# Second layer of a two-layer encoder kernel: another order of the attention units, the output projection begun with other rows, three numbers of the planner changed

## Chip, cores and metric

The kernel runs on one core of a Trainium2 chip. The metric is the time of one execution in device microseconds (us); lower is better. The time before is the median of three runs.

## The reference, cut to what matters

Two token sequences (1024 and 512 real tokens, each with 16 meta tokens in front, so 1040 and 528 rows, 1568 in all) go through two layers of width 1024 in float32:

```python
def layer(x, ...):
    h = rmsnorm(x, pre_g)
    proj = einsum('bld,de->ble', h, w_in)             # 1024 -> 3328 columns
    aq, ak, av, ag, bq, bk, bv, bg = parts
    oa = window_gqa_attention(rope(aq), rope(ak), av, sink) * silu(ag)   # 8 heads, 2 groups
    ob = diff_attention(rope(bq), rope(bk), bv, lam, ...) * silu(bg)     # 4 heads of 2 softmaxes
    o = einsum('ble,ed->bld', concatenate([oa, ob], axis=-1), w_out)
    return x + rmsnorm(o, post_g)
```

Sliding attention (`oa`): 8 query heads in 2 groups share a key head per group; a query sees the 16 meta tokens, keys up to 128 positions away on either side, and a sink. Differential attention (`ob`): 4 heads, each the difference of two full softmaxes over the whole sequence, applied to values of width 128, then normalised per row. The mixed rows are 512 of sliding and 512 of differential attention; the output projection multiplies all 1024 with `w_out`.

## The kernel before, in words

Every matmul works on float32 numbers split into a high and a low part, so each product is three matmuls. Tokens are cut into four chunks of 392; the input projection has 26 blocks of 128 columns. A differential head needs four blocks (two of queries and keys, values, gate); sliding group 0 needs six (keys and values of both groups among them), group 1 four.

A layer has six **units**: differential heads b0 to b3, `attn_b`, and sliding groups a0 and a1, `attn_a`. `units[0..3]` are the heads, `units[4]` and `units[5]` the groups. `UNITS[l]` gives the order in layer l. The main loop records, for each unit in that order, first its attention and then the input projection (`inproj`) of the unit that comes next: so dense matmuls of the next unit stand beside the attention of this one. After the last unit `outproj` is recorded. Its steps stand in `OUT_ORDER`: `first` (letter b) multiplies one half of the mixed rows with `w_out` for all chunks and keeps the partial sums; `second` (s, or S with weights not kept) adds the other half, then normalises, adds the residual and stores. `FH[l]` says which half `first` takes: 0 is the sliding rows, 1 the differential rows. Each half is 4 column blocks x 12 token tiles x 12 matmuls = 576 matmuls in layer 1.

Results pass between steps through DRAM: `AQ`, `AK`, `AV` (sliding queries, keys, values), `BS`, `BV` (differential), `GT` (gates), `MX` (mixed rows). All transfers are issued from one queue, SP's.

Nothing of this order is final. A `Recorder` writes every instruction down as an `Op` with a number `prio` (its place in the recording, less a boost and less a base), and `schedule()` deals them out to the engines beforehand: whenever an engine is free, it takes the ready op of lowest `prio`. What runs on the chip is that fixed order on each engine. `BASE[l]` holds the bases of the output projection's steps by their letter, `BASE_A[l]` those of the attention units by their place in the order (not by the unit); in layer 1 it is `(0, 0, 0, 0, 1500, 300)`, so places 5 and 6 are drawn forward.

Some ops can run on either of two engines (`any_copy`: ScalarE or VectorE; `any_tt`: VectorE or GpSimd). They stand on both lists, and `ANY` is added to their `prio` on one engine's list:

```python
def push(o):
    for e in o.alts:
        heapq.heappush(ready[e], (o.prio + (ANY[e] if len(o.alts) > 1 else 0), o.seq, o))
```

Buffers that matter: `slot` (16; the normalised input of the four chunks fills all of them as high and low parts until the last input projection has read it; then the mixed rows and the partial sums of `first` use them), `kk` and `vv` (one each: keys and values of a sequence; the next unit's can only be loaded when this one's are done), `qq` (2), `pp` (4), `whl` (2, split weights), and the PSUM pools `ps_s` (1: scores), `ps_t` (2), `ps_o` (1), `ps_d` (2: dense). With weights kept, `second` puts two of its four weight blocks into `kk` and `vv`, behind the last op of the last attention unit (`after[0]`). In the attention units the buffers of `ps_s`, `kk`, `qq`, `vv`, `pp`, `at`, `og` and `gl` are taken in recorded order, so units do not overtake each other.

In the trace all instructions have line L448, the line of the planner that issues them; tiles tell what they are.

Of the kernel before, what the change touches and what calls it, by code (L numbers as in the profile page):

```python
# [54 lines left out]
SPARE = (0, 0)  # L55
GROUPS = (((0, 1), (2, 3)), ((0, 1), (2, 3)), ((0, 1), (2, 3), (4, 5)))
COMB = ((1, 1, 1, 1), (1, 1, 1, 1))
BASE = ({'f': 400, 'p': 100, 's': -100, 'S': 0, 'b': 800, 'g': -50}, {'f': 0, 'S': 400, 'l': 1000})
BASE_A = ((-200, 1500, 1500, -200, 200, 400), (0, 0, 0, 0, 1500, 300))
FH = (1, 1)  # L60
UNITS = ((0, 1, 2, 3, 4, 5), (0, 1, 2, 3, 4, 5))


def even_tiles(t0, n, m):
# [57 lines left out]
ENG = ("PE", "ACT", "DVE", "POOL", "SP")  # L122
PE_COL = 0.0004453
PE_SWITCH = 0.39
ANY = {'PE': 0, 'ACT': 20, 'DVE': 0, 'POOL': 0, 'SP': 0}
POOL_MAX = 300


# [107 lines left out]
class Recorder:  # L236
# [89 lines left out]
    def schedule(self):  # L326
# [16 lines left out]
# [4 lines that stand above are left out]
# [193 lines left out]
def hymba_kernel(ctx, tc, xT, xr, w_in, w_out, rope, masks, pre_g, post_g, sub_g, sink_b, sink_m, lam_in, yo):  # L540
# [244 lines left out]
    def load_w(src, pool=None, pri=0):  # L785
        nc.boost = BOOST_W + pri * 100000
        nc.extra = [after[0]] if pool and after else []
        raw = (p_p if pri or pool and after else wraw_p)([128, 1024])
        dma(raw, src)
        nc.boost = BOOST_W  # L790
        w = (pool or whl_p)([128, 2, 8, 128], F32R)
        rv = raw.rearrange("p (a c) -> p a c", a=8)
        nc.any_copy(w[:, 0], rv)
        nc.any_tt(w[:, 1], rv, f32(w[:, 0]), ALU.subtract)
        nc.extra = []
        nc.boost = 0
        return w
# [502 lines left out]
    def load_mix(l, ci, half, small=False):  # L1300
        nc.boost = BOOST_M
        his, los = [], []
        k = 2 if small else 4
        n = sum(m for _, m in OCH[ci])
        for r0 in range(4 * half, 4 * half + 4, k):
            if ci == 4:
                hi, lo = [at_p([128, 4, n], F32R) for _ in range(2)]
            else:
                hi, lo = [p_p([128, 2, CN], F32R) for _ in range(2)] if small else pair(F32R)
            o = 0  # L1310
            nc.extra = [after[0]] if small else []
            for (t0, m) in OCH[ci]:
                dma(lo[:, :, o:o + m], SC[l]["MX"][r0:r0 + k, :, t0:t0 + m].rearrange("e p t -> p e t"))
                o += m
            nc.extra = []
            nc.any_copy(hi[:, :, 0:n], f32(lo[:, :, 0:n]))
            nc.any_tt(lo[:, :, 0:n], f32(lo[:, :, 0:n]), f32(hi[:, :, 0:n]), ALU.subtract)
            his.append(hi)
            los.append(lo)
        nc.boost = 0  # L1320
        return rows(his, k), rows(los, k)
# [4 lines left out]
    def outproj(l):  # L1326
# [18 lines left out]
        def first(*cs_):  # L1345
            for ci in cs_:
                mix[ci] = load_mix(l, ci, FH[l])
                if ci < 4:
                    part[ci] = halves([128, 3, 512])
            for dp in range(4):  # L1350
                w = load_w(w_out[l, FH[l], dp])
                u, c0 = dp // 2, 256 * (dp % 2)
# [16 lines left out]
        def load(ci):  # L1369
            mix[ci, 1] = load_mix(l, ci, 1 - FH[l], ci == 3 and l > 0)  # L1370

        def second(*cs_, keep=True):
# [9 lines left out]
            def get(dp):  # L1382
                if dp not in kept:
                    w = load_w(w_out[l, 1 - FH[l], dp], (None, None, k_p, v_p)[dp] if keep else None)
                    if keep:
# [95 lines left out]
        for step in OUT_ORDER[l].split():  # L1481
            nc.base = BASE[l].get(step[0], 0)
            for c in ([step[1:]] if step[0] in "bsS" else step[1:] or [""]):
# [41 lines left out]
    for l in range(NL):  # L1525
        order = [units[u] for u in UNITS[l]]
        es = [(e, pool, START.get(f"w{i}", 0) if l == 0 else 0)
# [70 lines left out]
```

## Time and profile before

| | |
|---|---|
| time, median of 3 runs | 1920.6 us (1920.0 to 1920.7) |
| time of the profiled execution | 1922.3 us |
| its span, first to last instruction | 1920.5 us |
| TensorE (PE) busy in the span | 1840.4 us, 96% |
| VectorE (DVE) busy | 1487.8 us, 77% |
| ScalarE (ACT) busy | 1028.0 us, 54% |
| mean granted clock of TensorE | 0.99 |

The span is what the trace covers; the time has 1.8 us more around it. The first layer takes about the first half. In layer 1 the differential heads run to about 1562 us, the sliding groups from about 1578 to 1838, and the second half of the output projection from there to the end. PE is matmuls, PEld the weight loads that run beside them, SP the queue that issues transfers; a number in brackets behind a timeline row is idle time of the engine before it and what ended it.

### The profile page before, as it was taken

The page shows a single profiled execution, that of the slowest core. Times are in us where ns is not written, and L with a number is a line of the kernel's source. Part 1 is how long each engine was busy: PE and PEld are TensorE (multiplying, and loading weights), DVE is VectorE, ACT ScalarE, POOL GpSimd, SP SyncE. Part 2 cuts the span into 40 slices and gives each one's busy share as a digit, 9 for nine tenths or more (in the row PEclk, how much of TensorE's full clock was granted, in tenths as well). Part 3 has the DMA queues.
Part 4 walks back from the last instruction along what each step waited for, and adds up shares of the span by engine and source line. Part 5 has one row for each costly group of instructions (what it writes and reads, how often), then busy time and mean ns, then how long its engine had stood idle before and what let it go on. Part 6 is the DMA issues. An engine that isn't in the chain of part 4 may idle for free.

```text
span 1920.5 us, 35745 instructions
## 1 busy us (share of the span) xinstructions
PE 1840.4 (96%) x12400; PEld 1772.5 (92%) x12400; DVE 1487.8 (77%) x3353; ACT 1028.0 (54%) x2458; POOL 267.7 (14%) x521
## 2 busy tenths in 40 slices
PE   7999999999999998998799999999999999989998
PEld 7999999999999898898699999999999999889998
DVE  7577787888796887676987387887968859879777
ACT  8345454465554666565664255454546537658642
POOL 2011111212121110010220021111211111101101
PEclk9999999999999998999899999999999999999999
DMA  8444453634545665655454444445453475684374
GB/s 252 133 107 125 132 135 110 165 84 131 155 101 148 158 163 135 148 140 147 154 182 115 134 119 136 130 118 156 109 167 107 125 174 127 157 221 115 84 238 150
DMA packets 296498, 273.04 MB, mean 142 GB/s; under 512 B 100822, under 2 KB 259670, under 8 KB 296190
## 3 DMA queue, kind: packets, MB, share of 16 engines
q1 hardware_dynamic: 296318, 270.76, 51.0%
q8 instruction: 99, 1.62, 0.4%
q14 instruction: 81, 0.66, 0.1%
HBM read 149.19 MB, written 96.01 MB: 128 GB/s over the span
## 4 chain that ended last, share of the span: by engine, by line
PE 72%; DMA 10%; DVE 9%; issue 3%; ACT 3%; SPq 3%; POOL 1%; DVEq 0%; POOLq 0%; ACTq 0%
PE ps_d L448 44%; PE ps_s L448 10%; PE ps_o L448 9%; PE ps_t L448 9%; SPq L448 3%; DVE at L448 2%; DVE pp L448 2%; DVE slot L448 2%; DMA slot<-MX 1%; ACT pp L448 1%; DMA kk<-AK 1%; DVE whl L448 1%; DVE sm L448 1%; DVE og L448 1%; DMA wraw<-in_w_in_dram 1%
## 5 line engine op out<-in xcount | busy, mean ns | idle before, releaser
L448 PE MATMUL ps_d<-slot,whl 128*128 128x392 f32 (+2 forms) x4560 | 939.9, 346 | 16.2 <-ACT slot L448 6.9
L448 PEld LDWEIGHTS ps_d<-slot,whl 128*128 128x128 f32 x4560 | 782.6, 189 | 23.8 <-ACT slot L448 6.8
L448 PE MATMUL ps_s<-kk,qq 128*128 128x264 f32 (+9 forms) x1496 | 284.5, 319 | 21.4 <-DMA qq<-qq 6.5
L448 PE MATMUL ps_o<-at,vv 128*128 128x256 f32 (+6 forms) x1368 | 284.7, 306 | 5.8 <-DVE og L448 2.6
L448 ACT ACTIVATE at<-ps_t 128x256 fp32r<-128x256 f32 (+10 forms) x426 | 184.7, 440 | 195.9 <-PE ps_t L448 170.9
L448 DVE TENSOR_TENSOR at<-ps_t,at 128x256 fp32r<-128x256 f32 (+6 forms) x472 | 225.3, 481 | 78.7 <-ACT at L448 63.9
L448 PE MATMUL ps_d<-whl,slot 128*128 128x256 f32 x1800 | 263.7, 291 | 16.2 <-DVE slot L448 10.9
L448 ACT ACTIVATE pp<-ps_s,sm 116x1040 f32<-116x1040 f32 (+4 forms) x208 | 204.0, 981 | 131.9 <-DVE sm L448 120.7
L448 PEld LDWEIGHTS ps_s<-kk,qq 128*128 128x128 f32 (+4 forms) x1496 | 226.3, 184 | 45.2 <-issue 9.4
L448 PEld LDWEIGHTS ps_d<-whl,slot 128*128 128x128 f32 x1800 | 238.3, 194 | 22.8 <-DVE slot L448 13.3
L448 ACT ACTIVATE pp<-pp,sm 128x336 f32<-128x336 f32 (+6 forms) x347 | 207.5, 611 | 91.8 <-DVE sm L448 88.8
L448 DVE TENSOR_REDUCE sm<-ps_s 116x1 f32<-116x1040 f32 (+4 forms) x208 | 218.5, 1051 | 47.4 <-PE ps_s L448 46.0
L448 PEld LDWEIGHTS ps_o<-at,vv 128*128 128x128 f32 (+1 forms) x1368 | 213.8, 189 | 13.2 <-DVE at L448 3.7
L448 PE MATMUL ps_t<-ident,pp 128*128 128x128 f32 (+6 forms) x1280 | 206.3, 268 | 3.6 <-ACT pp L448 2.0
L448 PEld LDWEIGHTS ps_t<-ident,pp 128*128 128x128 f32 (+6 forms) x1280 | 151.1, 137 | 14.2 <-ACT pp L448 2.6
L448 POOL TENSOR_TENSOR pad<-pp,pad 128x64 fp32r<-128x64 f32 (+5 forms) x148 | 54.4, 372 | 756.4 <-ACT pad L448 410.2
L448 POOL TENSOR_TENSOR sm<-sm 128x2 f32<-128x2 f32 (+3 forms) x112 | 51.0, 456 | 466.8 <-DVE sm L448 439.3
L448 DVE CUSTOM_DVE_ANT_0 pp<-ps_s,mk,nsinks 128x336 f32<-128x336 f32 (+2 forms) x192 | 97.2, 527 | 19.5 <-PE ps_s L448 17.8
L448 POOL TENSOR_TENSOR sm<-sm,mhalf 128x1 f32<-128x1 f32 (+6 forms) x107 | 82.5, 783 | 165.5 <-DVE sm L448 162.5
L448 ACT ACTIVATE og<-ps_o 64x128 f32<-64x128 f32 (+4 forms) x248 | 66.7, 287 | 45.2 <-PE ps_o L448 29.2
L448 ACT ACTIVATE ru<-ps_d 128x392 f32<-128x392 f32 (+5 forms) x101 | 49.0, 486 | 73.3 <-PE ps_d L448 62.5
L448 DVE CAST at<-ps_t 128x256 fp32r<-128x256 f32 (+9 forms) x142 | 69.7, 491 | 18.7 <-PE ps_t L448 16.3
(157 smaller groups left out, 2115.6 us busy)
## 6 DMA issues: line engine op xcount, KB each, us to landing
wraw<-in_w_in_dram SPq DMA_DIRECT2D x46, 512.0 KB
qq<-qq SPq DMA_DIRECT2D x144, 128.0 KB
BS<-st SPq DMA_DIRECT2D x64, 196.0 KB
qq<-AQ SPq DMA_DIRECT2D x96, 128.0 KB
gl<-GT SPq DMA_DIRECT2D x72, 128.0 KB
MX<-og SPq DMA_DIRECT2D x72, 128.0 KB
slot<-MX SPq DMA_DIRECT2D x11, 768.0 KB
kk<-BS SPq DMA_DIRECT2D x8, 1040.0 KB
```

Of the source, the lines that this page charges most:

```text
L448: fn(*[_real(a) for a in args], **{k: _real(a) for k, a in kw.items()})
```

## The change

In layer 1 the order of units becomes b0, a0, b1, a1, b2, b3 (before: b0, b1, b2, b3, a0, a1). `first` of layer 1 takes the sliding rows, `second` the differential ones. `BASE_A[1]` is not edited, so its 1500 and 300 now belong to b2 and b3 in places of a0 and a1. In layer 0 the base of step `S` (`second` on chunks 0 and 1) goes from 0 to 200. In both layers an op that can run on ScalarE or VectorE stands 380 places forward on ScalarE's list, where it stood 20 places back. No op is added or removed by any of it.

```diff
-BASE = ({'f': 400, 'p': 100, 's': -100, 'S': 0, 'b': 800, 'g': -50}, {'f': 0, 'S': 400, 'l': 1000})
+BASE = ({'f': 400, 'p': 100, 's': -100, 'S': 200, 'b': 800, 'g': -50}, {'f': 0, 'S': 400, 'l': 1000})
 BASE_A = ((-200, 1500, 1500, -200, 200, 400), (0, 0, 0, 0, 1500, 300))
-FH = (1, 1)
-UNITS = ((0, 1, 2, 3, 4, 5), (0, 1, 2, 3, 4, 5))
+FH = (1, 0)
+UNITS = ((0,1,2,3,4,5), (0,4,1,5,2,3))
...
-ANY = {'PE': 0, 'ACT': 20, 'DVE': 0, 'POOL': 0, 'SP': 0}
+ANY = {'PE': 0, 'ACT': -380, 'DVE': 0, 'POOL': 0, 'SP': 0}
```

## Rows read from the trace of the kernel before

**Rows 1.** The page: busy time of each engine, and busy tenths in 40 slices.

```profile
PE 1840.4 (96%) x12400; PEld 1772.5 (92%) x12400; DVE 1487.8 (77%) x3353; ACT 1028.0 (54%) x2458; POOL 267.7 (14%) x521
...
PE   7999999999999998998799999999999999989998
...
DVE  7577787888796887676987387887968859879777
```

**Rows 2.** Stages: length, then busy us (count) of each engine, PEclk, DMA.

```profile
600.00:900.00 300.00, 280.40 (x2000) 267.24 (x1998) 225.63 (x670) 179.08 (x516) 29.62 (x64) 0.98 0.59 151
900.00:1000.00 100.00, 85.47 (x618) 81.52 (x619) 88.80 (x193) 65.91 (x171) 23.92 (x30) 0.90 0.48 156
...
1110.00:1562.00 452.00, 446.89 (x2946) 433.87 (x2945) 360.98 (x720) 237.77 (x504) 74.24 (x156) 1.00 0.48 132
1578.00:1657.00 79.00, 77.31 (x497) 72.44 (x495) 68.43 (x211) 56.58 (x166) 9.73 (x17) 1.00 0.51 127
1657.00:1717.00 60.00, 53.11 (x325) 49.63 (x326) 46.85 (x121) 34.35 (x88) 4.61 (x10) 1.00 0.82 214
1717.00:1795.00 78.00, 76.83 (x578) 72.49 (x579) 64.05 (x201) 54.00 (x167) 10.85 (x20) 0.98 0.49 122
1795.00:1838.00 43.00, 42.53 (x347) 41.40 (x348) 31.37 (x104) 28.36 (x88) 1.66 (x4) 1.00 0.48 131
1838.00:1908.00 70.00, 68.41 (x568) 67.42 (x567) 53.58 (x84) 23.08 (x50) 9.32 (x10) 1.00 0.59 202
1908.00:1920.50 12.50, 5.29 (x45) 5.09 (x43) 7.23 (x13) 2.17 (x6) 1.85 (x2) 0.80 0.23 85
```

**Rows 3.** Chain of work that ended last, 1550 to 1850: start, us, what.

```profile
1690.33 8.20 DMA slot<-MX
...
1711.14 5.73 DMA kk<-AK
```

**Rows 4.** PE in order of time, 1655 to 1720, two rows with idle before.

```profile
1694.11 0.33 PE L448 MATMUL ps_t<-ident,pp 128*128 128x128 f32 x1 [1.88 <-ACT pp L448]
...
1717.01 1.16 PE L448 MATMUL ps_s<-kk,qq 128*128 128x208 f32 x6 [1.95 <-DMA kk<-AK]
```

**Rows 5.** SP's queue: b3's last two stores, first mixed-row load, last store.

```profile
1546.17 0.33 SPq L448 DMA_DIRECT2D MX<-og  x1
...
1562.83 0.33 SPq L448 DMA_DIRECT2D MX<-og  x1
...
1685.24 0.45 SPq L448 DMA_DIRECT2D slot<-MX  x1
...
1837.07 0.37 SPq L448 DMA_DIRECT2D MX<-og  x1
```

**Rows 6.** Groups by form, 1578 to 1700 (sliding): busy us, mean ns, idle before.

```profile
L448 ACT ACTIVATE pp<-pp,sm 128x336 f32<-128x336 f32 x46 | 25.4, 568 | 7.9 <-DVE sm L448 7.6
...
L448 ACT ACTIVATE at<-ps_t 128x512 fp32r<-128x512 f32 x17 | 9.9, 592 | 1.3 <-PE ps_t L448 1.0
...
L448 DVE TENSOR_SCALAR pp<-pp,sm 128x336 f32<-128x336 f32 x18 | 6.7, 417 | 0.1
...
L448 DVE CAST at<-ps_t 128x512 fp32r<-128x512 f32 x3 | 2.1, 685 | 0.7 <-PE ps_o L448 0.7
```

**Rows 7.** Groups by form, 1110 to 1562 (differential heads).

```profile
L448 DVE TENSOR_REDUCE sm<-ps_s 128x1 f32<-128x1040 f32 x60 | 74.1, 1236 | 10.4 <-PE ps_s L448 9.7
...
L448 ACT ACTIVATE pp<-ps_s,sm 128x1040 f32<-128x1040 f32 x60 | 67.7, 1128 | 27.1 <-DVE sm L448 23.1 <-POOL ru L448 3.2 <-POOL pad L448 0.3
```

**Rows 8.** Groups of the whole span: the weight blocks' first copy.

```profile
L448 ACT ACTIVATE whl<-wraw 128x1024 fp32r<-128x1024 f32 x40 | 42.1, 1053 | 17.5 <-DMA wraw<-in_w_in_dram 14.1 <-DMA wraw<-in_w_out_dram 2.8 <-PE ps_d L448 0.5
...
L448 DVE CAST whl<-wraw 128x1024 fp32r<-128x1024 f32 x22 | 15.1, 687 | 4.5 <-PE ps_d L448 4.4
```

**Rows 9.** Waits of PE, 900 to 1000: us, times, longest.

```profile
PE ps_d L448 <- DVE slot L448: 9.0, 8, 3.2
```

**Rows 10.** Chain of work that ended last, 1838 to the end.

```profile
1840.39 7.17 DMA pp<-in_w_out_dram
...
1884.10 23.49 PE ps_d L448 x195
```

## The prediction

> **What bounds the kernel now.** I read the page's busy shares first. PE is busy 1840.4 of 1920.5 us, with nine tenths or more in most slices; DVE follows with 77%, ACT with 54% [rows 1]. The change adds and removes no op, so the work of PE stays; only its idle time, 80.1 us in all, can shrink or grow. Next I read stages, to see where that idle time lies [rows 2]. In the differential heads of layer 1 (1110 to 1562) PE idles 452.0 - 446.9 = 5.1 us, 1.1 per 100. In the two sliding groups behind them (1578 to 1838, four rows) it idles 1.7 + 6.9 + 1.2 + 0.5 = 10.2 us in 260, two thirds of it in the one stretch 1657 to 1717. The final product (1838 to 1908) idles 1.6 us, the 12.5 us behind it are the last tile's normalisation and stores. Layer 0's counterpart is worse: 300.0 - 280.4 = 19.6 us at 600 to 900 and 100.0 - 85.5 = 14.5 us at 900 to 1000. The remaining 22 us or so lie in the start, the last tile and in stretches that the change touches only through ScalarE's list.
>
> So nothing here is worth more than some tens of us, and in layer 1 the reachable part is about 15.
>
> **What stops PE between 1657 and 1717.** I read PE's own order and the chain there. Group a1's input projection, the last of the layer, runs out while a0's four last blocks are still at work. The next dense work is `first`, and its mixed rows can be fetched only once the input's `slot` buffers are free: issued from 1685.24 on [rows 5], and 8.2 us for the second load [rows 3]. PE meanwhile has only the attention chain, and stops 1.9 us for an `exp` or a scaling [rows 4]. Then a1's keys must wait for a0's to be done (one `kk` buffer): 5.7 us [rows 3], with 1.95 us of PE idle at the end [rows 4]. The reader should see one cause in both: the reserve of dense work ran dry exactly where one sliding group hands over to the next.
>
> **The order of units, and `FH`.** Each unit keeps its instructions. What changes is its neighbour. The six blocks of a0 now stand beside b0 rather than b3, both differential heads, so this is a swap. a0 stands beside b1's four blocks (it had a1's four), a1 beside b2's four (it had `first`), and `first` moves from a1 to b3. `first` is 576 matmuls, at 23.49/195 = 0.1205 us each [rows 10] 69.4 us. An input projection of four blocks is of about the same size: 4 x 4 x 24 matmuls, of 392 columns instead of 256, so 1.53 times 0.1205, 71 us by my estimate from that row. PE's balance in each place is nearly unchanged.
>
> The place where the reserve runs dry moves from a0's end to b2's end and b3's start. All four differential heads ran with 1.1 us per 100 of idle time, but they always had hidden input projection ready. I bound the term: if b3's start covers it, as the heads' usual rate says, the 60 us would cost 0.7 rather than 6.9, a gain of 6.2; if it falls together with b3's own load of keys and queries, the same 6.9 is paid there, and the loads of sliding keys (5.7 us) could be exposed again at two new hand-overs, a loss of at most 2 x 1.95 = 3.9. The last block of an input projection frees its chunks one after the other, so part of the mixed rows arrives early, and the two sliding hand-overs now have an input projection beside them. I take half of the first bound: **-3.0**, between -6.2 and +3.9. SP issues the same transfers; the sliding keys and values now queue between the differential heads' query loads, which costs nothing while PE has dense work (that is the cover) and up to those 3.9 us if not.
>
> **The end.** `second` waits for the last unit: two weight blocks go into `kk` and `vv` behind its last store, a load of 7.17 us [rows 10] that the remaining dense products hide today, all but the 1.6 us above. The last store came at 1837.07, and the end 83.4 us later [rows 5]. With b3 last, the last stretch is longer: its last group of 256 queries came 1562.83 - 1546.17 = 16.7 us after the one before [rows 5], while sliding blocks finish in about (1795 - 1717)/8 = 9.8 us [rows 2]. Where dense products remain, the difference of 7 us is covered. If `first` is used up by then, PE has only the attention's own few us in it. Bounds 0 and +12 (16.7 less some 5 us of PE's own work); I take **+2.0**, near cover, because the planner puts attention ahead of dense work, and `second` has products for the two weight blocks in `whl` that need not wait.
>
> **ScalarE's list.** The shift from +20 to -380 lets ACT take a copy before an `exp` of up to 380 places earlier, and takes copies from DVE. In the sliding stage 1578 to 1657 DVE is busy 68.4 of 79 us, 87%, ACT 56.6, 72% [rows 2]; here relief is real. What can move there: scalings of 336 columns at 0.417 us on DVE (18 of them), against at most 0.568 us on ACT (the row mixes them with `exp`), and copies of 512 columns at 0.685 against 0.592 [rows 6]. All 18 and the 3 would free 9.6 us of DVE for at most 12.0 us of ACT. But PE's idle time in the three sliding stretches besides the dry one is only 3.4 us: I take half, **-1.5**, between -3.4 and the loss priced below. In a differential head the chain per softmax of 1040 is a minimum of 1.236 us and an `exp` of 1.128 [rows 7]; 16 of them are 38 us of a head's 113 us (452/4). A copy of 0.6 us ahead of each would add 10 us to that chain, hidden by the dense work that keeps PE full: nothing, and +5 at most for the four heads where the cover thins.
>
> **Layer 0.** `S` 200 places earlier stands only against the output projection's own later steps, so by itself it is worth little. Its surroundings are not: at 900 to 1000 PE waits 9.0 us for DVE's additions into the partial sums [rows 9], with DVE busy 88.8 of 100 us and ACT 65.9 [rows 2]. There ACT's taking copies meets the wait that ends last. I take half of 9.0 and 1.5 more in the sliding stage before it: **-6.0**, between -15 (all of 9.0, and 6 of the 19.6) and +6 (a sixth of the 34 us again, from an order that merely falls out differently).
>
> **Sum.** -3.0 + 2.0 - 1.5 - 6.0 = -8.5. The profiled execution took 1922.3, so 1913.8; it lies 1.7 above the median, so **1912** against 1920.6 us.
>
> **Rivals.** *The dry place only moves.* b3 pays the 6.9 us, the end +2, the layer 0 term nothing: 1920 to 1922, no change. For it speaks that each unit's dense neighbour is of equal size. *More is gained:* layer 0's -15 and layer 1's -6.2 and -3.4, no loss at the end: -24.6, about 1897. Against it: it needs every bound at once. *The end stands bare, slower:* b3's last group finds `first` used up. From the point where `first` ends more than about 17 us before b3's last store, the whole +12 is paid; if also the dry place keeps its 6.9 and layer 0 gives nothing, 1920.6 + 12 = 1933, with half of my gains 1928. For it: after b2 dense work is the scarcest, and the last head's chain is the longest. *ScalarE falls behind, slower:* every `exp` of the four sliding units waits for one copy of 0.592 us per block, 12 x 0.592 = 7.1 us per unit, 28 for four, and dense work hides about two thirds: +9, 1930. It decides once ACT's share of the sliding stage passes 90%, from 72; the moves above bring it to (56.6 + 12.0)/79, 87%, at most, which speaks against it.
>
> On ScalarE's list the rows cut both ways: the weight blocks' copy takes 1.053 us on ACT and 0.687 on DVE, from SBUF [rows 8], while the copy of 512 columns out of PSUM is the quicker on ACT [rows 6]. The Trainium skill, page "ScalarE: Activation LUTs", section "Rules for kernel authors", says to use VectorE and not ScalarE for adds and multiplications, which is against this edit. The trace agrees for the weight blocks and disagrees for the copies out of PSUM. By the rule alone the edit would give only the last rival's loss, 1930 us; by the rows the sum above.
>
> **Chances and range.** The forecast, 1905 to 1917: 0.45. More gained, 1890 to 1905: 0.13. No change: 0.17. Bare end: 0.14. ScalarE behind: 0.11. A measurement of this kernel can tell about 0.2%, 3.8 us, from no change. So faster 0.58, same 0.17, slower 0.25. For 8 in 10, I leave out the lower half of the second case and the upper half of the two slow ones: 1899 to 1930. The likeliest one's own range is 1905 to 1917.
>
> **What would show it.** In the profile after: PE's idle time between a0 and a1's ends below 2 us per 100 (order right); a stretch of some 7 us idle around b3's first keys (only moved); the last `MX` store later than about 83 us before the end, or PE idle over 5 us in the last 100 us (bare end); DVE's total down and ACT's up by 20 us or more, with ACT's share in sliding stages under 90% (list right); PE's wait for DVE's additions at the end of layer 0 near 4 us rather than 9.0. I am wrong if layer 0 grows, or if PE's total idle time, 80.1 us now, does not fall by about 8.

## The result and the profile after

The changed kernel took 1934.7 us (median of five runs, 1930.1 to 1937.3) against 1920.7. These two medians have the quotient 1.0073; the ratio on record, which the text uses throughout, is 1.0055, with an interval from 1.0039 to 1.0072. A second timing beside other experiments gave 1.0068 (1.0044 to 1.0091). It is slower by about 0.6%; I had forecast 1912 us, 0.45% faster, and a range that ended at 1930. The profiled execution was the quickest of the five: 1930.1 us, with a span of 1928.3, 7.8 us more than before. So its trace shows a little over half of the loss in the medians.

The page after, busy time of each engine (before: [rows 1]):

```profile
PE 1841.9 (96%) x12400; PEld 1768.1 (92%) x12400; DVE 1473.2 (76%) x3293; ACT 1045.4 (54%) x2509; POOL 272.7 (14%) x530
```

PE's idle time rose from 80.1 to 1928.3 - 1841.9 = 86.4 us, where I had wanted a fall of 8. DVE's total fell by 14.6 us, ACT's rose by 17.4. Next both kernels cut at 1110 us, where nearly the same number of matmuls is done (the columns are those of [rows 2]); first before, with its stretch 1000 to 1110, then after:

```profile
0.00:1110.00 1110.00, 1056.59 (x7030) 1017.00 (x7031) 852.18 (x1897) 588.89 (x1385) 155.41 (x303) 0.99 0.51 141
1110.00:1920.50 810.50, 783.83 (x5372) 755.46 (x5370) 635.66 (x1457) 439.08 (x1073) 112.26 (x219) 0.99 0.52 143
...
1000.00:1110.00 110.00, 107.94 (x644) 104.88 (x643) 64.34 (x115) 38.42 (x66) 8.00 (x13) 1.00 0.45 128
```

```profile
0.00:1110.00 1110.00, 1053.49 (x7018) 1010.52 (x7019) 838.96 (x1850) 602.42 (x1430) 161.82 (x307) 0.99 0.51 142
1110.00:1928.30 818.30, 788.44 (x5384) 757.57 (x5382) 634.26 (x1444) 442.98 (x1079) 110.91 (x223) 0.99 0.51 141
```

At 1110 the changed kernel is 12 matmuls behind. The rest, layer 1 and those 12, takes 7.8 us more. Its stages after: end of layer 0 and hand-over (three rows), then b0, a0, b1, a1, b2, b3, the final product and the last tile:

```profile
600.00:900.00 300.00, 276.99 (x1937) 262.93 (x1936) 219.87 (x640) 173.37 (x511) 27.59 (x63) 0.98 0.59 148
900.00:1000.00 100.00, 90.53 (x707) 86.09 (x706) 91.03 (x205) 71.58 (x187) 24.11 (x30) 1.00 0.51 162
1000.00:1110.00 110.00, 103.84 (x616) 100.90 (x616) 60.73 (x111) 44.18 (x80) 7.72 (x11) 0.98 0.47 135
1110.00:1222.00 112.00, 109.41 (x710) 105.75 (x709) 86.24 (x179) 56.38 (x121) 18.59 (x40) 0.98 0.50 127
1222.00:1352.00 130.00, 125.17 (x781) 118.08 (x780) 97.27 (x299) 77.42 (x221) 13.55 (x26) 1.00 0.52 135
1352.00:1479.00 127.00, 126.26 (x830) 122.74 (x829) 102.91 (x204) 66.79 (x152) 16.70 (x35) 1.00 0.47 136
1479.00:1601.00 122.00, 116.38 (x735) 108.55 (x734) 95.47 (x293) 78.61 (x226) 15.28 (x35) 1.00 0.63 156
1601.00:1734.00 133.00, 130.09 (x867) 125.25 (x868) 112.61 (x220) 73.98 (x156) 19.58 (x40) 1.00 0.55 156
1734.00:1849.50 115.50, 115.07 (x943) 112.79 (x941) 84.21 (x163) 66.94 (x152) 16.30 (x37) 1.00 0.40 126
1849.50:1915.50 66.00, 61.42 (x493) 59.98 (x492) 48.40 (x77) 20.69 (x47) 9.05 (x10) 0.97 0.48 162
1915.50:1928.30 12.80, 4.64 (x40) 4.43 (x38) 7.15 (x13) 2.17 (x6) 1.86 (x2) 0.86 0.34 125
```

Read the first two numbers of a row: length less PE busy is idle time. Of layer 0's end one stretch improved: 900 to 1000 idles 9.5 us instead of 14.5 [rows 2]. Before it 600 to 900 idles 23.0 instead of 19.6, and behind it 1000 to 1110 idles 6.2 instead of 2.1. From 0 to 1110 PE idles 56.5 us against 53.4, so layer 0 gained nothing. The sliding stages idle 4.8 and 5.6 us, b2 2.9, b3 only 0.4, the final product 4.6. PE's longest stop behind the start is in layer 0, 4.14 us in front of 728.54. It, the one at the hand-over to layer 1 and the two behind b3's last store, in PE's order of time:

```profile
728.54 2.95 PE L448 MATMUL ps_d<-slot,whl 128*128 128x384 f32 x8 [4.14 <-DVE ru L448]
...
1006.79 1.02 PE L448 MATMUL ps_d<-slot,whl 128*128 128x392 f32 x2 [4.12 <-DVE slot L448]
...
1855.03 0.38 PE L448 MATMUL ps_d<-kk,slot 128*128 128x256 f32 x1 [2.54 <-ACT kk L448]
1856.29 4.51 PE L448 MATMUL ps_d<-kk,slot 128*128 128x256 f32 x23 [0.88 <-DVE kk L448]
```

In the second the input projection of layer 1 waits for the normalised input that DVE writes into `slot`. In the last two, behind the store of 1849.10, the weight block in `kk` is not split yet. The granted clock in these last two places, in the 10 us behind the first of them, and in single microseconds in, just behind and well behind that stop:

```profile
1000.00:1010.00 10.00, 5.88 (x28) 5.45 (x28) 9.48 (x22) 6.97 (x16) 4.00 (x4) 0.83 0.47 161
1010.00:1020.00 10.00, 10.00 (x68) 9.70 (x67) 6.38 (x11) 6.83 (x14) 0.54 (x1) 1.00 0.42 115
1850.00:1860.00 10.00, 6.58 (x41) 6.18 (x40) 6.21 (x8) 4.81 (x8) 0.00 (x0) 0.83 0.58 195
...
1005.00:1006.00 1.00, 0.00 (x0) 0.00 (x0) 1.00 (x3) 0.40 (x1) 0.00 (x0) 1.00 0.00 0
1008.00:1009.00 1.00, 1.00 (x7) 1.00 (x6) 0.52 (x3) 0.25 (x1) 0.54 (x1) 0.50 0.00 0
1012.00:1013.00 1.00, 1.00 (x9) 0.96 (x8) 0.48 (x1) 1.00 (x3) 0.00 (x0) 1.00 0.98 205
```

0.83 means that of its two levels, 2.4 and 1.2 GHz, PE had the lower one for part of these 10 us. The single rows say which part: 1.00 in the stop, 0.50 behind it, when PE worked again, then 1.00.

Last, PE's waits for transfers in the attention of layer 1, 1110 to 1838, before and after:

```profile
PE ps_s L448 <- DMA kk<-AK: 2.3, 2, 1.9
...
PE ps_s L448 <- DMA kk<-BS: 1.0, 2, 0.5
```

```profile
PE ps_s L448 <- DMA qq<-qq: 2.3, 3, 1.5
PE ps_s L448 <- DMA kk<-AK: 1.9, 2, 1.7
PE ps_s L448 <- DMA vv<-AV: 1.3, 1, 1.3
...
PE ps_s L448 <- DMA kk<-BS: 0.6, 1, 0.6
PE ps_o L448 <- DMA vv<-BV: 0.3, 1, 0.3
```

They went from 3.3 to 6.4 us. The wait at the end of layer 0 that the prediction named, PE for DVE's additions at 900 to 1000, was 9.0 us before [rows 9] and is now:

```profile
PE ps_d L448 <- DVE slot L448: 7.7, 7, 2.2
```

Two waits for ACT, which before has in the same stretch, are not there after:

```profile
PE ps_t L448 <- ACT slot L448: 2.3, 1, 2.3
PE ps_d L448 <- ACT slot L448: 1.9, 1, 1.9
```

### The profile page after: what moved, and what is told of

The parts are those of the page before. It is cut to its first block, busy times and chain, and to the rows that moved or that the text cites. A ratio compares the mean times of both kernels' runs of the same rounds, so it can differ in the third digit from the quotient of the medians.

```text
span 1928.3 us, 35805 instructions
## 1 busy us (share of the span) xinstructions
PE 1841.9 (96%) x12400; PEld 1768.1 (92%) x12400; DVE 1473.2 (76%) x3293; ACT 1045.4 (54%) x2509; POOL 272.7 (14%) x530
## 4 chain that ended last, share of the span: by engine, by line
PE 65%; DMA 12%; DVE 11%; ACT 4%; SPq 3%; issue 3%; POOL 0%; DVEq 0%; POOLq 0%; ACTq 0%
PE ps_d L448 39%; PE ps_s L448 9%; PE ps_o L448 9%; PE ps_t L448 8%; SPq L448 3%; DVE slot L448 2%; DVE pp L448 2%; DVE sm L448 2%; DVE at L448 1%; DMA slot<-MX 1%; ACT pp L448 1%; DMA vv<-AV 1%; DMA wraw<-in_w_in_dram 1%; DVE whl L448 1%; DVE og L448 1%
## 5 line engine op out<-in xcount | busy, mean ns | idle before, releaser
L448 PE MATMUL ps_o<-at,vv 128*128 128x256 f32 (+7 forms) x1368 | 285.2, 307 | 9.3 <-ACT at L448 3.5
L448 ACT ACTIVATE at<-ps_t 128x256 fp32r<-128x256 f32 (+12 forms) x442 | 190.0, 436 | 173.4 <-PE ps_t L448 147.2
L448 PE MATMUL ps_d<-whl,slot 128*128 128x256 f32 x1800 | 256.9, 287 | 11.0 <-DVE slot L448 10.8
L448 ACT ACTIVATE pp<-pp,sm 128x336 f32<-128x336 f32 (+8 forms) x362 | 214.9, 609 | 79.1 <-DVE sm L448 74.6
L448 PEld LDWEIGHTS ps_d<-whl,slot 128*128 128x128 f32 x1800 | 231.2, 190 | 15.6 <-DVE slot L448 9.9
L448 PEld LDWEIGHTS ps_o<-at,vv 128*128 128x128 f32 (+1 forms) x1368 | 212.2, 189 | 19.6 <-DVE at L448 5.6
L448 POOL TENSOR_TENSOR sm<-sm 128x2 f32<-128x2 f32 (+2 forms) x112 | 46.8, 419 | 508.4 <-DVE sm L448 493.6
L448 POOL TENSOR_TENSOR sm<-sm,mhalf 128x1 f32<-128x1 f32 (+7 forms) x107 | 83.8, 791 | 148.1 <-DVE sm L448 144.6
L448 ACT ACTIVATE ru<-slot 128x512 f32<-128x512 f32 (+1 forms) x82 | 51.2, 625 | 53.6 <-DVE slot L448 51.6
```

Of the source, the lines that this page charges most:

```text
L448: fn(*[_real(a) for a in args], **{k: _real(a) for k, a in kw.items()})
```

## The experiments

Each ratio is against the kernel before on the same chip; chips differ by some us, so medians of different groups are not compared. A trace is one execution, and executions of one kernel differ: the nineteen of the kernel before beside e1 to e4 took 1916.2 to 1932.1 us.

**One edit at a time.** e1 takes the two lines `FH` and `UNITS` of the diff, e2 the line `ANY`, e3 the line `BASE`, e4 `ANY` and `BASE`.

> The new order of units and the new half for the first product alone; bases and ScalarE's list as before. If the order costs (the last head's bare end and the later start of layer 1), 1928 to 1935 us, with PE idle about 3 to 4 us behind the last store of mixed rows. If ScalarE's list costs, within 3 us of 1920.7. If every re-dealing of the ops simply lands elsewhere, any value within some 10 us, not equal to the change's loss.

> ScalarE's list at -380 alone, order and bases as before. If the list costs, 1926 to 1935 us; if the order costs, 1917 to 1923 us, with VectorE's total 10 to 20 us lower and ScalarE's as much higher, and the wait for VectorE's additions at the end of layer 0 below 9.0 us.

> The base of step S in layer 0 at 200 alone. It should change only the stretch 900 to 1000: 1917 to 1924 us by each theory. A difference of more than 4 us would speak for scatter from any re-dealing.

> ScalarE's list and the base of S together, the order as before, so the whole change but its order. If the order costs, 1915 to 1923 us; if the list costs, 1926 to 1935; if scatter, a value that is not the sum of the two single edits.

| kernel | ratio | interval |
|---|---|---|
| e1, order and half | 1.0067 | 1.0046 to 1.0087 |
| e2, ScalarE's list | 1.0081 | 1.0052 to 1.011 |
| e3, base of S | 0.9984 | 0.9968 to 1.0 |
| e4, list and S | 1.0114 | 1.008 to 1.0149 |

By these ratios the order alone and the list alone each cost as much as the whole change or more. Three single effects of +0.67, +0.81 and -0.16% sum to +1.3%, and the whole is +0.6%: the terms do not add. Both theories that put the loss into one edit fall. Where the two lost time, 1110 us to the end, order (e1) and list (e2):

```profile
1110.00:1929.70 819.70, 790.99 (x5361) 755.49 (x5359) 635.88 (x1435) 436.82 (x1074) 116.94 (x222) 0.99 0.51 141
```

```profile
1110.00:1934.40 824.40, 787.54 (x5354) 757.55 (x5352) 635.60 (x1445) 436.26 (x1081) 108.97 (x211) 0.99 0.51 140
```

For the order the stretch is 9.2 us longer than before's 810.5, but PE's idle time only 28.7 against 26.7. The weight loads tell more: idle 819.7 - 755.5 = 64.2 against 810.5 - 755.5 = 55.0 us, so 9.2 more. This is many short gaps, which the overlapping records of matmuls cover, and not one stop: counted in the two traces behind the first 7030 matmuls, weight loads had 42 gaps of 0.3 to 1 us (20.7 us in all) against 19 (9.5 us) before, and 9 longer ones against 11. With the list alone PE's own idle time shows more of it, 36.9 us.

**Is the kernel before an uncommonly close fit?** A dealing is here the fixed order on each engine that `schedule()` arrives at, and a close fit one that leaves few gaps. e5, e6 and f4 leave all of the change out and shift each op's place in layer 1 at random:

```diff
-            o.prio = o.seq - self.boost - self.base + self.rnd.random() * SPREAD
+            o.prio = o.seq - self.boost - self.base + self.rnd.random() * self.spread
...
+        nc.spread = 8 if l == NL - 1 else 0      # seeds 36, 37 and 41
```

> The kernel before, with every op's place in layer 1 shifted at random by 0 to 8 places, and nothing else. If the order or ScalarE's list costs by a mechanism of its own, this stays within 4 us of the kernel before. If the dealing of the kernel before is simply an uncommonly close fit and any other dealing loses, 1928 to 1942 us on the scale of 1921 to 1924 for the kernel before, with PE's idle time and stretches at half clock up by several us in layer 1.

> The same shift at random with another seed. If a mechanism, within 4 us of the kernel before; if any other dealing loses, again 5 to 20 us slower, by an amount that differs from the first seed's, with the waits in other places.

> The kernel before with every op's place in layer 1 shifted at random by 0 to 8 places, a third seed. If any other dealing loses, 1.002 to 1.010 again, which makes three of three; a ratio under 1.001 would say that the kernel before is no uncommon fit.

They gave 1.0034 (1.0015 to 1.0054), 1.0073 (1.0049 to 1.0096) and 1.0041 (1.0027 to 1.0056). Three of three are slower, by amounts like those of the edits, though a shift of at most 8 places among thousands has no aim at all. Their stretch from 1110 to the end, and below them that of e8, which comes further down and has a ratio of 1.0:

```profile
1110.00:1936.30 826.30, 795.45 (x5403) 763.71 (x5401) 643.98 (x1475) 438.06 (x1073) 109.42 (x213) 0.99 0.51 141
```

```profile
1110.00:1936.30 826.30, 790.09 (x5365) 758.01 (x5363) 637.20 (x1451) 429.55 (x1072) 116.04 (x222) 0.99 0.50 140
```

```profile
1110.00:1930.60 820.60, 794.93 (x5416) 761.46 (x5414) 644.47 (x1465) 442.10 (x1082) 109.77 (x219) 1.00 0.51 143
```

```profile
1110.00:1929.90 819.90, 788.29 (x5377) 758.04 (x5375) 632.17 (x1433) 440.90 (x1089) 110.22 (x218) 1.00 0.51 142
```

Weight loads idle 62.6, 68.3 and 59.1 us, all more than 55.0; the change's 60.7 lies among them. But so does e8's 61.9, so this number alone does not say that a kernel is slower. And the third row holds 44 matmuls more than before's (x5416, x5372): f4 was late at 1110 already, though its matmuls stand in before's order up to the 6443rd.

e9 puts the same shift (seed 37) on the changed kernel.

> The changed kernel with every op's place in layer 1 shifted at random by 0 to 8 places (the second seed of before). If the changed kernel is one dealing among many, this lies as far from the kernel before as the shifted kernels before did, ratio 1.003 to 1.010, above or below the change's own 1.0055. If its order and list cost by mechanisms of their own and its dealing is as close a fit as that of before, the shift adds another 0.3 to 0.7%: ratio 1.009 to 1.013.

It gave 1.0089 (1.0063 to 1.0115), some 0.3% over the change: inside the first forecast and at the lower edge of the second one's 1.009. So it does not decide whether the changed dealing is a close fit too.

**The two halves of ScalarE's list.** e7 gives -380 to ops of the attention units alone, e8 to dense work's alone:

```diff
-... (ANY[e] if len(o.alts) > 1 else 0) ...
+... ((-380 if e == "ACT" and o.stream == "attn" else ANY[e]) if len(o.alts) > 1 else 0) ...   # e8: != "attn"
```

> ScalarE's list at -380 for the ops of the attention units alone (copies of turned probabilities, scalings); dense work's copies stay at +20. If the loss of 16 us of the whole edit comes from copies that delay an exp in the attention units, most of it is here, 1932 to 1942 us; if it comes from dense work's copies that push ahead of the exps, this is within 4 us of the kernel before; if any other dealing loses, both halves lose and do not add up to the whole.

> ScalarE's list at -380 for the dense work's copies alone. If these push ahead of the exps and cost, 1932 to 1942 us; if the attention units' copies cost, within 4 us of the kernel before; if any other dealing loses, slower by 5 us or more as well.

1.004 (1.0024 to 1.0056) and 1.0 (0.9982 to 1.0018). Together they make 1.0081, so these do not seem to add either, though 0.4 to 0.8% is hardly more than the intervals. The half of the attention units costs something, that of the dense work, the weight blocks' copies among it, nothing that can be told. The totals of the two traces, e7 and then e8:

```profile
sum 1933.60, PE 1845.78 PEld 1774.96 DVE 1491.20 ACT 1027.02 POOL 263.04; mean PE 922.89 PEld 887.48 DVE 745.60 ACT 513.51 POOL 131.52
```

```profile
sum 1929.90, PE 1842.55 PEld 1772.25 DVE 1479.97 ACT 1037.18 POOL 273.89; mean PE 921.27 PEld 886.12 DVE 739.99 ACT 518.59 POOL 136.94
```

Against DVE's 1487.8 and ACT's 1028.0 before [rows 1], the half that costs has moved no work to ACT, and the half that has moved 9 us to it costs nothing. So in these traces the cost does not go with work moved to ACT.

**The number of hand-overs.** e10 has the groups side by side, else it is e1:

```diff
-UNITS = ((0,1,2,3,4,5), (0,4,1,5,2,3))
+UNITS = ((0,1,2,3,4,5), (0,1,4,5,2,3))
```

> Order b0, b1, a0, a1, b2, b3 with the new half for the first product, all else as before: two hand-overs between sliding and differential units fewer than in the change, the last head still at the end. If the exposed loads at the alternating hand-overs are the cost of the order, ratio 1.000 to 1.004 where the order alone had 1.0067. If any other dealing loses, 1.003 to 1.010, in no relation to the number of hand-overs.

1.0074 (1.0045 to 1.0103): with two hand-overs fewer no better than the order's 1.0067. That the alternation as such is the cost is not borne out.

**The base of S.** e11 and f2 are the change without its line `BASE`, f1 is the change itself beside f2, f3 the order with S, e12 S alone once more.

> The changed kernel with the base of step S back at 0; few instructions differ. If S and ScalarE's list together make the stop of 4.1 us at the hand-over to layer 1, this stop is gone, with the half clock behind it, and the kernel is 4 to 7 us faster than the changed one: ratio to before 1.001 to 1.004. If S has no part, ratio 1.0055 and the stop still there.

> The changed kernel again, beside its version without S on the same chip. If S causes most of the change's loss, the ratio is 1.004 to 1.007 and stays 0.3 to 0.5% above the version without S; if the difference between them came from the chip, both have the same ratio.

> The changed kernel with S back at 0, on the same chip. If S causes most of the loss, 0.999 to 1.003; if the chip did, 1.004 to 1.007, the same as the change.

> The order and the first product's half with S at 200, ScalarE's list as before. If S costs only together with ScalarE's list, this is at or a little below the order alone (1.0067), 1.004 to 1.007, and has no stop of 4.1 us at the hand-over; if S costs with any other dealing, 1.009 to 1.012.

> The base of step S at 200 alone once more, in five rounds, as the only edit so far with a ratio below 1 (0.9984, from 0.9968 to 1.0). If it is a gain, 0.997 to 0.999 with an interval under 1; if scatter of the chip, 0.999 to 1.001.

| kernel | ratio | interval | stop of over 4 us at 1006 to 1012 |
|---|---|---|---|
| change | 1.0055 | 1.0039 to 1.0072 | yes |
| f1, change again | 1.0068 | 1.0044 to 1.0091 | yes |
| e11, without S | 1.0013 | 0.9991 to 1.0036 | no |
| f2, without S again | 1.0038 | 1.0022 to 1.0054 | no |
| f3, order and S | 1.005 | 1.0033 to 1.0066 | no |
| e12, S alone again | 0.9982 | 0.9964 to 1.0 | no |

Of all profiles, the four that have both S and the list (the change, f1, e4 and e9) have the stop, and no other. f2's 1.0038 lies between its two forecasts, so S causes a part of the loss and not most of it. PE in order of time, f1 and then e4:

```profile
1009.36 1.02 PE L448 MATMUL ps_d<-slot,whl 128*128 128x392 f32 x2 [4.13 <-DVE slot L448]
```

```profile
1012.24 1.02 PE L448 MATMUL ps_d<-slot,whl 128*128 128x392 f32 x2 [4.12 <-DVE slot L448]
```

S without the list has a stop of this length too, 50 us earlier, in the last products of layer 0: 4.03 us in e3, 4.80 in e12, and 4.34 in f3, the row below; before's longest there is 3.17. Yet without the list S gains, so one stop does not tell what an edit costs.

```profile
957.82 0.80 PE L448 MATMUL ps_d<-whl,slot 128*128 128x256 f32 x2 [4.34 <-ACT slot L448]
```

The input that PE waits for in the changed kernel was transposed by PE and its high part written by ACT long before the stop:

```profile
991.37 1.04 PE L448 MATMUL ps_t<-ident,slot 128*128 128x128 f32 x8
```

```profile
992.35 1.05 ACT L448 ACTIVATE slot<-ps_t,preg 128x392 fp32r<-128x392 f32 x2
```

What DVE does meanwhile, in order of time, up to the end of PE's stop at 1006.79:

```profile
997.01 1.23 DVE L448 TENSOR_TENSOR whl<-wraw,whl 128x1024 fp32r<-128x1024 f32 x1 [0.84 <-ACT whl L448]
...
1003.55 0.62 DVE L448 SCALAR_TENSOR_TENSOR rw<-ps_d,scl,cs 128x392 f32<-128x392 f32 x1
...
1005.10 1.03 DVE L448 TENSOR_TENSOR ru<-ru,rw 128x392 f32<-128x392 f32 x2
...
1006.11 1.16 DVE L448 SCALAR_TENSOR_TENSOR slot<-ps_t,preg,slot 128x392 fp32r<-128x392 f32 x2
```

Its low part, the last row, comes 13 us after the high one. On DVE it stands behind a weight block's low part (`whl`), layer 0's last normalisations and layer 1's first rope products (`rw`, `ru`).

With the list, S costs 0.33% (e4 over e2) and 0.30% (f1 over f2); without it S gains about 0.17% (e3, e12, f3 against e1). None of these differences is clearly wider than its intervals, but all agree in sign, and the traces agree where S acts: from the 5901st matmul to the 7031st the four with S and the list take 185.2 to 186.2 us, the three with the list alone (e2, e11, f2) 180.6 to 183.4. Behind that PE's order is the same with S and without.

S alone is the best version met: 0.9984 and 0.9982, both intervals ending at 1.0.

**Layer 1 counted by work.** A cut at a fixed time gives each kernel another amount of work. So here is the time of all that follows the first 7030 matmuls, worked out from each kept trace, with the number of gaps of 0.3 to 1 us between weight loads in it. Kernels parted by a comma have the same order on PE there, those parted by a semicolon do not.

| dealing of layer 1 | kernels | us | gaps |
|---|---|---|---|
| before's | before, e3, e12 | 810.5, 811.4, 811.3 | 19, 20, 23 |
| the change's | change, f1, e11, f2 | 816.0, 818.1, 812.9, 815.6 | 36, 37, 34, 30 |
| order alone | e1, f3 | 821.7, 821.6 | 42, 40 |
| list alone | e2, e4 | 827.0, 827.8 | 30, 31 |
| groups side by side | e10 | 822.7 | 33 |
| halves of the list | e7; e8 | 821.2; 819.4 | 25; 31 |
| random shifts | e5; e6; f4 | 820.8; 827.4; 812.3 | 36; 38; 37 |
| change, shifted | e9 | 823.4 | 40 |

None of the ten other dealings is shorter than before's in these traces, and each has more of these gaps, 25 to 42 against 19 to 23. Traces of one dealing differ by up to 5.2 us, so f4's 1.8 us are within that. The ratios say the same but for e8: its trace, the slowest of its ten executions, is 8.9 us longer here, its ratio 1.0.

**The granted clock as a rival.** Among the nineteen executions of the kernel before beside e1 to e4, the slower ones have the lower mean granted clock (the quickest 0.993, the slowest 0.987). By a straight line through them, an estimate, 0.001 of mean clock goes with about 1.4 us; which of the two brings the other is not shown. e1's nine have 0.0009 less on average, e2's five 0.0015 less: 1 to 2 us of their 13 and 16. By this estimate the clock is not the main cause. But e8 and e11 have 0.0021 and 0.0032 more than before beside them, some 3 and 5 us by like estimates, so their ratios near 1 may owe something to it; f2, e11's kernel again, has 0.0009 more and 1.0038.

## Why the prediction was wrong

The step that failed is the sum, and in it first the two terms of ScalarE's list and layer 0, -1.5 and -6.0. I priced each edit as a local move in the dealing that the trace of before shows, and put the re-dealing of everything else at nothing in layer 1; "an order that merely falls out differently" had a bound of +6 in layer 0 alone. The runs showed in its place:

- The order alone costs 0.67%, some 13 us, where its terms were -3.0 and +2.0. The list alone costs 0.81%, some 16 us, where I had -1.5 and most of -6.0. Together they cost less than either, so the terms do not add.
- Shifts of layer 1 without any aim cost 0.34 to 0.73%, 6 to 14 us, as much as any term of mine and more. That is a term which belonged on top of the sum. Not every re-dealing costs as much: e8, whose matmuls leave before's order at the 220th, had a ratio of 1.0.

Term by term:

- **ScalarE's list, -1.5.** The move itself came: DVE fell by 14.6 us and ACT rose by 17.4 (20 was my mark). But the list alone costs 0.81%. I had taken DVE's 87% in the sliding stage for a limit whose relief PE would feel; DVE fell to 97.3/130 = 75% and 95.5/122 = 78% there, and PE did not idle less. The rival by which ScalarE falls behind is not what happened either: its share in the sliding stages is 77.4/130 = 60% and 78.6/122 = 64%, far from 90%, and the half of the edit that gives ACT more work costs nothing that can be told. That rival's 1930 us are near the result by luck, not for its reason. The Trainium skill, page "ScalarE: Activation LUTs", section "Rules for kernel authors", says to use VectorE and not ScalarE for adds and multiplications. No run here shows its price by itself: e7, the half with the scalings, moved no work to ACT in total.
- **Layer 0, -6.0.** At 900 to 1000 PE's idle time fell by 5.1 us, about as said, but not by the wait that I had named: PE's wait for DVE's additions went from 9.0 to 7.7 us, where my mark was 4; what went away is mostly 4.2 us of waits for ACT. And the gain came back, as 3.4 us more at 600 to 900 and 4.1 more at 1000 to 1110, the latter mostly the stop of 4.12 us. I had called S by itself worth little, since it stands only against the projection's later steps. With the list and S, DVE still has weights, normalisations and rope products to write when PE needs the next chunk's input.
- **The order, -3.0.** The dry place did move to b2's end, and it cost less there: b2 idles 2.9 us in 133 and b3 0.4, against 6.9 in 60 before [rows 2]. The gain was given back in the sliding stages: 10.4 us in 252, where the three besides the dry one had 3.4 in 200. All of layer 1's attention idles 17.1 us against 26.7 - 1.6 - 7.2 = 17.9, so PE's idle time gives this term -0.8. Waits for loads rose by 3.1 us over the whole attention; my bound for those at the new hand-overs was +3.9, and I had not taken it, because an input projection stood beside them. But alone the order costs 0.67%, and e1's trace has most of that in short gaps of the weight loads, which a sum over PE's idle time does not hold.
- **The end, +2.0.** Right in kind, larger in size: the final product idles 4.6 us against 1.6 [rows 2], the last tile 8.2 against 7.2, so +4.0, with the clock at its lower level for part of it. The weight blocks wait for b3, and products in front of them were used up 3.4 us early. My sign for a bare end, over 5 us of idle time in the last 100, could not tell: before has 1.6 + 7.2 there.

I gave "slower" 0.25, for a bare end or a late ScalarE. The first came with 4 of its 12 us, the second not. What stays open is the cause in layer 1: why order and list, 0.67 and 0.81% alone, make only 0.13 to 0.38% together (e11, f2). By the count of work this lies in layer 1 itself, 11 and 17 us alone and 2 to 8 together. That the kernel before is an uncommonly close fit, by chance or by choice, would explain it, and none of ten other dealings was shorter; but three shifts and one shift of the change are too few to tell chance from a mechanism. Giving the last two weight blocks buffers of their own, which would have measured the end by itself, was not tried.

Two slips in the working change nothing: the remaining 22 us do not hold the last tile, whose 7.2 come on top, and -24.6 us make 1896, not 1897.

## What to carry to other kernels

When a planner deals out all ops beforehand and PE is busy 96%, price an edit of its numbers as a new draw: a small random shift of the places, three times, tells what a draw costs here, and an edit must beat that. Do not sum single gains whose places share one dealing; S gained a little alone and cost a little beside the list. Compare traces from the same matmul on and not from the same time, take a second trace of the same kernel as the measure of scatter, and read the idle time of weight loads beside that of matmuls before saying where a loss lies.

## What the runs showed of the hardware

Matmul busy time can hide a loss. With the order alone the stretch from 1110 on took 9.2 us more, PE's idle time only 2.0 more, its weight loads' idle time 9.2 more; with the list alone these were 13.9, 10.2 and 11.8. The Trainium skill, page "Trainium Kernel Development and Optimization", section "Performance Expectations", calls matmul busy time a bad metric for how close a kernel is to roofline, because matmuls are pipelined, and the busy share of weight loads a good one. The rows of the order agree: there the weight loads show what matmul busy time does not.

The granted clock was 0.83 over the 10 us that hold the stop at 1007 and over those that hold the stops at 1855. By single microseconds it was 1.00 in the first stop and 0.50 when PE worked again behind it; where PE had stayed busy, as at 1012, it was 1.00. So a stop cost more than its own length here: by these rows an estimate of up to (1 - 0.83) x 10 = 1.7 us each.
